# Hybrid decoder trunk on one core: gate and output steps with one engine per step, pre-split output weights, other buffers for the keys' weights

## The chip, the cores and the metric

The kernel runs on one core of a Trainium2 chip, as one program. The core has a matrix engine (PE, whose weight loads are listed apart as PEld), a vector engine (DVE), an activation engine (ACT), a general engine (POOL) and 16 DMA engines; nearly all transfers are issued in order by one queue, SP. Each engine takes its instructions in program order and waits for others on semaphores. The metric is the device time of one execution in microseconds; the median of the runs counts. A change of 0.2% is about 5 us here.

## What is computed

Two layers on x of 1024 tokens by 1024 features, all float32. Layer 0 has a dilated attention, layer 1 a gated linear attention (GLA: 4 heads, keys of 128, values of 256, chunks of 64), each followed by a squared-ReLU MLP of width 4096. Cut to what the change touches:

```python
def gla_mixer(h, w_in, w_gate_up, b_gate, norm_w, w_out):
    proj = h @ w_in                                  # q, k, v, g_out, gate_lr
    gk = gate_lr @ w_gate_up + b_gate
    log_a = jax.nn.log_sigmoid(gk) / 16.0
    b = jnp.cumsum(chunked(log_a), axis=-2)
    q_t, k_t = qc * jnp.exp(b), kc * jnp.exp(-b)
    A = causal(q_t @ k_t)                            # scores of a chunk
    U = (kc * jnp.exp(b_last - b)).T @ vc            # update of the state
    o = A @ vc + q_t @ state
    o = rmsnorm(o, norm_w) * jax.nn.silu(g_out)
    return o @ w_out

def sq_relu_mlp(h, w_up, w_down):
    a = jax.nn.relu(h @ w_up)
    return (a * a) @ w_down

for i in range(2):
    x = x + mixer[i](rmsnorm(x, norm_mix_w[i]))
    x = x + sq_relu_mlp(rmsnorm(x, norm_mlp_w[i]), mlp_w_up[i], mlp_w_down[i])
return rmsnorm(x, final_norm_w)
```

## The kernel before

**Numbers.** Every float32 operand is split into a high part and a remainder (ACT copies the high part, DVE subtracts), and a product is three matmuls of 128 x 128 weights by 512 columns. The large products go through a scheme of seven block products in place of eight, whose operands are sums and differences of blocks (a11, a12, s1 to s4, a22).

**Stages.** In order of time: attention's projection (0 to 275 us), its heads (to 870), its output projection (to 1075), the MLP of layer 0 with Up (to 1300) and Down (to 1600), the keys of the GLA with the gates of heads 0 and 1 (to 1720), the GLA's values and output gate (the object `gates`, to 1880), the two head pairs of the GLA beside its output projection (to 2050), and the MLP of layer 1 (Up to 2340, Down to the end).

**What sets the order.** The order is that of the code. Stages with a clock call `at(t, fn, priority)`, and a function runs when the clock reaches its step; `tick()` moves a clock and takes the next function of the list `steps`, so that work of ACT, DVE, POOL and SP is written between blocks of matmuls. Within a step an engine's instructions stand in the order of the calls. Tiles come from pools with a fixed number of buffers: `k4` (25 buffers of 4 KB for each partition), `t2` (8 of 2 KB), `h8`, `r6`, and eight PSUM banks. A new tile waits until the earlier user of its buffer is done, a store's landing included.

**Up of layer 0.** `Up.run` goes over 16 blocks p of seven products s (12 matmuls each). Beside product (p, s) it writes, in this order: what becomes of the product before (`done`: e is ACT's copy of pX, c11, c12 and rb are DVE's sums, then ACT's Relu and Square on them), and `stage(p + 1, s)`, which splits a piece of the next block's weights. c12 is squared ahead of the stage of s = 0, and rb ahead of that of s = 6. The object `Trickle` splits the GLA's key weights meanwhile, for later use: `Trickle.step` runs in the steps of even p + s for 4 <= p < 15, 3.5 times in each p. One head takes nine such steps: load, nothing, then cuts (ACT copies `th`, DVE subtracts `tl` one step later, SP stores both into `wp`) with differences (`less`, DVE) in the same step as the cut that reads them. `th` and `tl` are `t2` tiles, as are e and c.

**GLA gates.** `Gate` makes the decays of a head and half: first (ACT Abs, DVE min, ACT Exp and Ln, POOL subtract), second (DVE scan, POOL, three ACT Exp), third (three ACT Exp, DVE), keys, store. `Silu` makes silu of the output gate, eight pieces: load of z, first (ACT Exp, DVE add), then second (two ACT: Ln, Exp) and third (three DVE) in one step, then a store to `gscr`. All eight run in the steps of the product of `gates`.

**Pairs and output projection.** `Pair.scores(j)` makes the scores of four token blocks (16 matmuls of 128 columns in two calls of eight) into bank pA, `output(b)` makes the output of token block b for two heads, each head's matmuls followed by ACT's Square of that head (`gj`) for the norm; `flush` ends block b as `gy`, and `turn` transposes it. `Pair.load_keys` loads eight key tiles, `load_gates` the silu values. The output projection `out_proj(1)` first adds the product of heads 0 and 1, then that of heads 2 and 3. Its weights are the eight 128-row pieces of g_out: `Weights` (W) loads each raw, ACT scales it by the norm's weight into `whi`, and DVE forms `wlo`; its `prep` does so for one piece, near the place of use.

Of the kernel before, what the change touches and what calls it, by code (L numbers as in the profile page):

```python
# [19 lines left out]
P = 128  # L20
# [21 lines left out]
def hybrid_trunk(ctx, tc, x, norm_mix, norm_mlp, norm_fin, a_in, a_out, g_in, g_up, g_b, g_nw,  # L42
# [68 lines left out]
    class Weights:  # L111
        def __init__(self):
            self.slots = []
            self.scales = []
# [10 lines left out]
        def add(self, src, scale=None):  # L125
            self.slots.append(src)
            self.scales.append(scale)
# [9 lines left out]
        def prep(self, eng=pool):  # L137
            n = self.nprep
            while self.ndma <= n:
                self.dma()  # L140
            src, scale = self.raws.pop(n), self.scales[n]
            self.nprep += 1
            hi = k4(list(src.shape), F32R, "whi")
            lo = k4(list(src.shape), F32R, "wlo")
            if scale is None:
                act.activation(hi, src, AF.Copy)
                eng.tensor_tensor(lo, src, hi.bitcast(F32), op=OP.subtract)
            else:
                act.activation(hi, src, AF.Copy, scale=scale)
                dve.scalar_tensor_tensor(lo, src, scale, hi.bitcast(F32), op0=OP.mult, op1=OP.subtract)  # L150
            self.parts[n] = (hi, lo)

        def pump(self):
            while self.ndma < min(self.nprep + self.early, len(self.slots)):
                self.dma()
# [21 lines left out]
    def add_rows(w, k0, scale=None):  # L177
        for k in range(2):
            W.add(w[P * (k0 + k):P * (k0 + k + 1), :], None if scale is None else scale[:, k:k + 1])
# [428 lines left out]
    class Trickle:  # L608


        def __init__(self, out):
            self.out = out
            self.todo, self.behind = deque(), deque()
            for p in range(GH):
                self.plan(p)

        def plan(self, p):
# [9 lines left out]
            def cut(src, hi, lo, i, j):  # L627
                h, l = t2([P, 4, DK], F32R, "th"), t2([P, 4, DK], F32R, "tl")
# [11 lines left out]

            def three():
                less("b11", "b12", "b11")
                less("b12", "b22", "b12")
                cut("b11", "bh", "bl", 1, 1)

            def four():
                less("b22", "b22", "b11")
                cut("b22", "bh", "bl", 0, 0)

            def five():  # L650
                less("b21", "b21", "b22")
                cut("b12", "gh", "gl", 0, 0)
            self.todo.extend((load, lambda: None,
                              lambda: cut("b11", "ah", "al", 0, 0),
                              lambda: cut("b21", "ah", "al", 1, 1),
                              lambda: cut("b22", "d", "d", 0, 1),
                              three, four, five, lambda: cut("b21", "gh", "gl", 1, 1)))
# [16 lines left out]
    class Up:  # L674
# [165 lines left out]
        def run(self, tail):  # L840
# [44 lines left out]
    wpre = [[[drp.tile([P, 1024], F32, name=f"wp{i}_{p}_{n}") for n in PARTS] for p in range(AHEAD)] for i in range(3)]  # L885

# [657 lines left out]
    def out_proj(layer, wbc_row, o, up):  # L1544
# [10 lines left out]
        def add_block(tb, lhs, w, n, quiet=False):  # L1555
            last = tb == NB - 1 and n == 1
            ps = bank("pd")
            for k in range(4):
# [3 lines left out]
                if last:  # L1562
                    W.free(1)
            xx = xs[tb // 2][:, tb % 2, 512 * n:512 * n + 512]
            dve.tensor_tensor(xx, ps, xx, op=OP.add)
            if quiet:
                W.pump()
            else:
                tick()

        for tb in range(NB):
# [3 lines left out]
            if tb == (NB - 1 if layer else 3):  # L1575
                W.limit = 6
                W.early = RAW
            for n in range(2):
                add_block(tb, lambda k: tuple(t[k // 2][:, k % 2, 128 * tb:128 * tb + 128] for t in oT), w, n, layer == 0 and tb == NB - 1 and n == 1)
# [221 lines left out]
    gm, bgate, gnw = masks[:, 0:128].bitcast(U32), masks[:, 128:132], masks[:, 132:134]  # L1801
    low = {}

    def gate_loads():
        sp.dma_start(gm, gmask)
        sp.dma_start(bgate, g_b[0].rearrange("(h p) -> p h", p=P))
        sp.dma_start(gnw, g_nw[0].rearrange("(k p) -> p k", p=P))
# [87 lines left out]
    class Gate:  # L1895
# [10 lines left out]
        def first(self):  # L1906
            z = logits(self.h, self.half) if self.z is None else self.z
            b = bgate[:, self.h:self.h + 1]
            am = k4([P, 2, 512], F32, "ga")
            a, m = self.a, self.m = am[:, 0, :], am[:, 1, :]  # L1910
            act.activation(a, z, AF.Abs, bias=b)
            dve.tensor_scalar(m, z, b, 0.0, op0=OP.add, op1=OP.min)
            act.activation(a, a, AF.Exp, scale=-1.0)
            act.activation(a, a, AF.Ln, bias=1.0)
            pool.tensor_tensor(m, m, a, op=OP.subtract)
# [8 lines left out]
        def second(self):  # L1924
            self.eb = k4([P, 2, 512], F32, "eb")
            self.es = t2([P, 512], F32, "es")
            dve.tensor_tensor_scan(self.a, reset, self.m, 0.0, op0=OP.mult, op1=OP.add)
            e_q, e_k, e_s, a_c, m_c = self.views()
            end = [a_c[:, c, :, CH - 1:CH].to_broadcast([P, 4, CH]) for c in range(2)]
            pool.tensor_tensor(m_c[:, 0], a_c[:, 0], end[0], op=OP.subtract)  # L1930
            pool.tensor_tensor(m_c[:, 1], end[1], a_c[:, 1], op=OP.subtract)
            self.exp(e_q[:, 1], a_c[:, 1], 1.0)
            self.exp(e_k[:, 1], a_c[:, 1], -1.0)
            self.exp(e_s[:, 0], a_c[:, 0], 1.0)

        def third(self):
            e_q, e_k, e_s, a_c, m_c = self.views()
            self.exp(e_q[:, 0], m_c[:, 0], 1.0)
            self.exp(e_k[:, 0], m_c[:, 0], -1.0)
            self.exp(e_s[:, 1], m_c[:, 1], 1.0)  # L1940
            d = self.d
# [4 lines left out]
        def keys(self):  # L1946
            bs = lambda t: t.rearrange("p (b s) -> p b s", s=P)
# [15 lines left out]
        def plan(self, t, gap):  # L1963
            at(t, self.first, 7)
            at(t + gap, self.second, 7)
            at(t + gap, self.load, 8)
            at(t + 2 * gap, self.third, 7)
            at(t + 3 * gap - (gap > 1), self.keys, 8)
            at(t + 3 * gap - (gap > 1) + 1, self.store, 9)

    class Silu:
# [9 lines left out]
        def first(self):  # L1981
            d = self.d = k4([P, 2, 512], F32, "gd")
            act.activation(d, self.z, AF.Exp, scale=-1.0)
            dve.tensor_scalar(d, d, 1.0, 3e38, op0=OP.add, op1=OP.min)
# [293 lines left out]
```

## Time and profile before

| | |
|---|---|
| median of 3 runs | 2681.62 us (2680.1 to 2682.46) |
| the profiled execution | 2679.75 us, span 2678.0 us |
| around the span | 1.75 us |
| mean granted PE clock | 0.994 |
| HBM read, written | 331.09 MB, 169.54 MB |

The profiled execution is 1.87 us below the median. The profile's busy time of PE is modelled: matmuls overlap, so PE may be called busy in a stretch that has fewer matmuls than another of the same length. The count of matmuls in a stretch tells more. A row of the wait view gives who waited for whom, the total, how many waits, and the longest. A row of the view by stretches gives the stretch, its length, and for PE, PEld, DVE, ACT and POOL the busy time with the count of instructions, then the granted PE clock (1.00 is full), the share of the DMA engines that was busy, and GB/s. The chain of waits gives start, length, and what ran.

### The profile page before, as it was taken

The page shows a single profiled execution, that of the slowest core. Times are in us where ns is not written, and L with a number is a line of the kernel's source. Part 1 is how long each engine was busy: PE and PEld are TensorE (multiplying, and loading weights), DVE is VectorE, ACT ScalarE, POOL GpSimd, SP SyncE. Part 2 cuts the span into 40 slices and gives each one's busy share as a digit, 9 for nine tenths or more (in the row PEclk, how much of TensorE's full clock was granted, in tenths as well). Part 3 has the DMA queues.
Part 4 walks back from the last instruction along what each step waited for, and adds up shares of the span by engine and source line. Part 5 has one row for each costly group of instructions (what it writes and reads, how often), then busy time and mean ns, then how long its engine had stood idle before and what let it go on. Part 6 is the DMA issues. An engine that isn't in the chain of part 4 may idle for free.

```text
span 2678.0 us, 33562 instructions
## 1 busy us (share of the span) xinstructions
PE 2600.7 (97%) x12096; PEld 2151.9 (80%) x12096; DVE 1881.7 (70%) x3010; ACT 1279.6 (48%) x2340; POOL 29.3 (1%) x32
## 2 busy tenths in 40 slices
PE   8999999999999999999999999998889999999998
PEld 6888888888888888777788888876668888888886
DVE  7766878888888665666668785876556566656567
ACT  6443455555555354555544453554324455553343
POOL 0000000000000000000000000300000000000000
PEclk9999999999999999999999999999999999999999
DMA  5675455565566557666788765776414644496543
GB/s 185 240 270 185 121 142 154 140 164 147 142 159 185 186 180 269 223 216 212 280 302 302 259 220 191 259 264 221 164 41 158 253 163 145 142 327 216 184 150 124
DMA packets 351223, 528.03 MB, mean 197 GB/s; under 512 B 23408, under 2 KB 179440, under 8 KB 351056
## 3 DMA queue, kind: packets, MB, share of 16 engines
q1 hardware_dynamic: 351056, 525.88, 59.8%
q8 instruction: 95, 1.56, 0.2%
q14 instruction: 72, 0.59, 0.1%
HBM read 331.09 MB, written 169.54 MB: 187 GB/s over the span
## 4 chain that ended last, share of the span: by engine, by line
PE 74%; DVE 11%; ACT 6%; DMA 4%; issue 4%; SPq 0%; DVEq 0%; ACTq 0%
PE pB L1675 13%; PE pX L768 12%; PE pA L1675 10%; PE pV L768 8%; PE pB L967 6%; PE pY L768 4%; PE pA L967 4%; PE pZ L768 4%; PE pd L194 2%; PE pd L195 2%; PE pd L193 2%; PE pS L1072 1%; PE pO L1113 1%; DMA cw<-c 1%; DVE c L1166 1%
## 5 line engine op out<-in xcount | busy, mean ns | idle before, releaser
L1675 PE MATMUL pB<-dh 128*128 128x512 f32 x512 | 199.4, 389 | 0.0
L1675 PE MATMUL pB<-dh,dl 128*128 128x512 f32 x512 | 199.4, 389 | 0.0
L1675 PE MATMUL pB<-dl,dh 128*128 128x512 f32 x512 | 199.4, 389 | 0.0
L202 DVE TENSOR_TENSOR dl<-sin,dh 128x1024 fp32r<-128x1024 f32 x112 | 136.8, 1221 | 66.1 <-ACT dh L199 63.5
L768 PE MATMUL pV<-s4h,wd 128*128 128x512 f32 x480 | 162.0, 400 | 3.1 <-DVE rb L793 1.5
L199 ACT ACTIVATE dh<-sin 128x1024 fp32r<-128x1024 f32 x112 | 117.8, 1052 | 79.8 <-PE pB L1675 26.8
L1088 ACT ACTIVATE pt<-pt,orow 128x128 f32<-128x128 f32 (+1 forms) x192 | 85.0, 443 | 148.2 <-DVE orow L1086 146.9
L1675 PE MATMUL pA<-dh 128*128 128x512 f32 x384 | 149.7, 390 | 0.0
L1675 PE MATMUL pA<-dh,dl 128*128 128x512 f32 x384 | 149.6, 390 | 0.0
L1675 PE MATMUL pA<-dl,dh 128*128 128x512 f32 x384 | 149.6, 390 | 0.0
L199 ACT ACTIVATE dh<-kept 128x1024 fp32r<-128x1024 f32 x64 | 67.8, 1059 | 147.0 <-DVE kept L1640 105.3
L773 ACT ACTIVATE e<-pX 128x512 f32<-128x512 f32 x108 | 63.6, 589 | 112.0 <-PE pX L768 101.8
L1675 PEld LDWEIGHTS pB<-dh 128*128 128x128 f32 x512 | 96.2, 188 | 20.0
L1675 PEld LDWEIGHTS pB<-dl,dh 128*128 128x128 f32 x512 | 96.2, 188 | 19.8
L1675 PEld LDWEIGHTS pB<-dh,dl 128*128 128x128 f32 x512 | 96.2, 188 | 19.8
L768 PEld LDWEIGHTS pV<-s4h,wd 128*128 128x128 f32 x480 | 90.2, 188 | 24.0 <-DVE rb L793 3.3
L706 DVE TENSOR_TENSOR wbl<-t,wbh 128x1024 fp32r<-128x1024 f32 x48 | 58.8, 1225 | 67.2 <-ACT wbh L705 67.2
L768 PE MATMUL pX<-s3h,wgh 128*128 128x512 f32 x240 | 98.9, 412 | 6.8 <-ACT e L773 6.7
L768 PE MATMUL pX<-s2h,wbh 128*128 128x512 f32 x240 | 97.1, 404 | 8.5 <-ACT e L773 8.5
L777 ACT ACTIVATE c<-c 128x512 f32<-128x512 f32 x64 | 40.4, 631 | 128.7 <-DVE c L805 79.9
L706 DVE TENSOR_TENSOR wal<-raw,wah 128x512 fp32r<-128x512 f32 x96 | 66.0, 687 | 44.8 <-ACT wah L705 44.8
L768 PE MATMUL pY<-a12h,wah 128*128 128x512 f32 x240 | 96.0, 400 | 0.0
(328 smaller groups left out, 7428.1 us busy)
## 6 DMA issues: line engine op xcount, KB each, us to landing
sin<-acts SPq DMA_DIRECT2D x112, 512.0 KB, 4.9
acts<-s SPq DMA_DIRECT2D x64, 512.0 KB, 3.5
raw<-in_mlp_w_down_dram SPq DMA_DIRECT2D x64, 512.0 KB, 5.3
raw<-in_attn_w_in_dram SPq DMA_DIRECT2D x96, 256.0 KB, 4.4
cw<-c SPq DMA_DIRECT2D x192, 128.0 KB, 2.3
raw<-in_mlp_w_up_dram SPq DMA_DIRECT2D x48, 512.0 KB, 6.1
acts<-c SPq DMA_DIRECT2D x64, 256.0 KB, 2.2
kept<-in_mlp_w_down_dram SPq DMA_DIRECT2D x32, 512.0 KB, 6.6
```

Of the source, the lines that this page charges most:

```text
L193: pe.matmul(ps, sh, mh, start=start, stop=False)
L194: pe.matmul(ps, sh, ml, start=False, stop=False)
L195: pe.matmul(ps, sl, mh, start=False, stop=stop)
L199: act.activation(hi, src, AF.Copy)
L202: dve.tensor_tensor(lo, src, hi.bitcast(F32), op=OP.subtract)
L706: self.remain(lambda: dve.tensor_tensor(lo, src, hi.bitcast(F32), op=OP.subtract))
L768: pe.matmul(st[b], u[:, k, :], v, start=first and k + n == 0, stop=k == 3 and n == 2, skip_group_check=True)
L773: act.activation(e, self.st[p]["X"], AF.Copy)
L777: act.activation(r, r, AF.Relu)
L967: pe.matmul(self.acc[s][t], a[:, c], b[:, k, :], start=fresh and m + k + v == 0, stop=m == 1 and k == 1 and v == 2, skip_group_check=True)
L1088: act.activation(pt[:, i, :128 * n], pt[:, i, :128 * n], AF.Exp, scale=-1.0, bias=m, accum_out=self.row[:, r, HD:HD + 1])
L1675: pe.matmul(self.acc[s][t], a[:, k, c], b[:, k, :], start=fresh and m + k + v == 0, stop=m == 7 and k == 1 and v == 2, skip_group_check=True)
```

## The change

In Up of both layers, c12 and rb are still summed ahead of the stage, but their Relu and Square come after it (`add` and `squared` called apart). `Trickle` puts both parts of a cut into one `k4` tile `tb`, does each `less` one step ahead of the cut that reads it, and runs at s >= 3 for every p >= 4, four times in each p. It now also loads the eight pieces of g_out (512 KB each), splits them (ACT with the norm's scale, DVE) and stores both parts into DRAM tiles `wout` (sixteen stores of 512 KB); two steps are added to its 36. `Weights.prep` of these pieces becomes two loads of 512 KB, without work for ACT or DVE; four pieces are asked for in one place, four more at the end of the first half of the output projection, whose last token block now runs both halves of the columns side by side (`last_block`). `Gate` and `Silu` are cut so that each step has work of one engine (or of DVE then POOL). The subtraction that POOL had in `Gate.first` is part of a DVE instruction, and ACT has one more instruction there. Three of the eight `Silu`s move from the steps of `gates` into those of the output projection. `scores` and `turn` come one step later, `turn` first. In `output` the matmuls of both heads come before both Squares. `one.flush()` comes ahead of the last product of `gates`.

```diff
         def prep(self, eng=pool):
             n = self.nprep
+            self.nprep += 1
+            if isinstance(self.slots[n], tuple):
+                self.ndma = n + 1
+                got = []
+                for src, name in zip(self.slots[n], ("whi", "wlo")):
+                    t = k4([P, D], F32R, name)
+                    sp.dma_start(t.bitcast(F32), src)
+                    got.append(t)
+                self.parts[n] = tuple(got)
+                return
...
-            else:
-                act.activation(hi, src, AF.Copy, scale=scale)
-                dve.scalar_tensor_tensor(lo, src, scale, hi.bitcast(F32), op0=OP.mult, op1=OP.subtract)
...
+        def rows(self, k):
+            if k < 0:
+                return
+            raw, scale = self.raw.pop(k), gnw[:, k % 2:k % 2 + 1]
+            both = [k4([P, D], F32R, n) for n in ("whi", "wlo")]
+            act.activation(both[0], raw, AF.Copy, scale=scale)
+
+            def rest():
+                dve.scalar_tensor_tensor(both[1], raw, scale, both[0].bitcast(F32), op0=OP.mult, op1=OP.subtract)
+                for t, to in zip(both, wout[k]):
+                    sp.dma_start(to, t.bitcast(F32))
+            self.behind.append(rest)
...
             def cut(src, hi, lo, i, j):
-                h, l = t2([P, 4, DK], F32R, "th"), t2([P, 4, DK], F32R, "tl")
+                both = k4([P, 2, 4, DK], F32R, "tb")
+                h, l = both[:, 0], both[:, 1]
                 act.activation(h, r[src], AF.Copy)
...
             def three():
-                less("b11", "b12", "b11")
+                cut("b11", "bh", "bl", 1, 1)
                 less("b12", "b22", "b12")
-                cut("b11", "bh", "bl", 1, 1)
+                less("b22", "b22", "b11")
...
-                    if s == first:
+                    if s == 0:
+                        self.add(p - 1, 6)
+                    elif s == first:
                         self.done(p - 1, 6)
...
-                    if s > first and (p, s) != (3, 3):
+                    if s == 6:
+                        self.add(p, 5)
+                    elif s > first and (p, s) != (3, 3):
                         self.done(p, s - 1)
                     self.stage(p + 1, s)
+                    if s == 0:
+                        self.squared(p - 1, 6)
+                    elif s == 6:
+                        self.squared(p, 5)
...
-                    if self.side is not None and 4 <= p < NP - 1 and (p + s) % 2 == 0:
+                    if self.side is not None and 4 <= p and s >= 3:
                         self.side.step()
...
+        def last_block(w):
+            ps = [bank("pd") for _ in range(2)]
+            for k in range(4):
+                a, b = (t[k // 2][:, k % 2, 128 * NB - 128:] for t in oT)
+                wh, wl = w[k]
+                for n in range(2):
+                    mm3(ps[n], a, b, wh[:, 512 * n:512 * n + 512], wl[:, 512 * n:512 * n + 512], k == 0, k == 3)
+                W.free(1)
                 W.pump()
...
-    for t, i, q in ((7, 0, 0), (9, 1, 0), (13, 0, 1), (15, 2, 0), (17, 3, 0), (19, 1, 1), (21, 2, 1), (23, 3, 1)):
+    for t, i, q in ((7, 0, 0), (9, 1, 0), (13, 0, 1), (15, 2, 0), (17, 3, 0)):
         Silu(i, q).plan(c + t)
...
                 pe.matmul(po[:, i, :], AM[i][:, b, :], self.v(i, b), start=b == 0, stop=True, skip_group_check=True)
+            for i in range(2):
                 junk = t2([P, DV], F32, "gj")
...
-                  (24, lambda: one.scores(0)),
-                  (25, lambda: (one.turn(0), one.scores(1))),
+                  (25, lambda: (one.turn(0), one.scores(0))),
+                  (26, lambda: one.scores(1)),
```

**ACT in Up of layer 0, before.** These rows are the head of one block p, from its product 0 on: c is the piece c12 of the block before (L777 is Relu, L778 Square), L705 are the weight splits of `stage`, L629 the cuts of `Trickle`, L773 the copies e.

```order
L777 ACTIVATE c_10254<-c_10254 128x512
L778 ACTIVATE c_10254<-c_10254 128x512
L705 ACTIVATE wah<-raw 128x512
L629 ACTIVATE th<-traw 128x512
L773 ACTIVATE e_10297<-pX 128x512
L705 ACTIVATE wah<-raw 128x512
L777 ACTIVATE c_10313<-c_10313 128x512
L778 ACTIVATE c_10313<-c_10313 128x512
L629 ACTIVATE th<-traw 128x512
L773 ACTIVATE e_10341<-pX 128x512
```

The same place of the changed kernel, where L732 are the splits, L804 and L805 Relu and Square, L800 the copies, L654 the cuts of `Trickle`:

```order
L732 ACTIVATE wah<-raw 128x512
L804 ACTIVATE c_10293<-c_10293 128x512
L805 ACTIVATE c_10293<-c_10293 128x512
L800 ACTIVATE e_10328<-pX 128x512
L732 ACTIVATE wah<-raw 128x512
L804 ACTIVATE c_10344<-c_10344 128x512
L805 ACTIVATE c_10344<-c_10344 128x512
L800 ACTIVATE e_10365<-pX 128x512
L732 ACTIVATE wbh<-t 128x1024
L654 ACTIVATE tb<-traw 128x512
L654 ACTIVATE tb<-traw_10052 128x512
```

The first split stands ahead of c12's squares, and the cuts stand behind the split of wbh, none of them before the first two copies e.

**DVE ahead of the first scores, before.** gd and ge are the tiles of a `Silu` (L1993 to L1995 its third step, L1984 its first), dl the remainder of a weight split (L952), kept and raw sums of weights (L922), V the finished values (L2016), whose bank the scores take.

```order
L1993 TENSOR_TENSOR gd<-gd,ge 128x1024
L1994 SCALAR_TENSOR_TENSOR ge<-gd,ge 128x1024
L1995 SCALAR_TENSOR_TENSOR ge<-gz,ge 128x1024
L952 TENSOR_TENSOR dl<-kept,dh 128x1024
L922 TENSOR_TENSOR kept<-kept 128x1024
L1984 TENSOR_SCALAR gd<-gd 128x1024
L952 TENSOR_TENSOR dl<-kept,dh 128x1024
L922 TENSOR_TENSOR raw<-raw,kept 128x1024
L2016 TENSOR_TENSOR V<-pB,c_15683 128x512
L2016 TENSOR_TENSOR V<-pB,c_15685 128x512
L1993 TENSOR_TENSOR gd<-gd,ge 128x1024
```

The same place of the changed kernel, with L2045 to L2047 for the fourth step of a `Silu`, L990 for dl, L960 for the sums, L2072 for V and L2130 for the masking of the scores:

```order
L2045 TENSOR_TENSOR gd<-gd,ge 128x1024
L2046 SCALAR_TENSOR_TENSOR ge<-gd,ge 128x1024
L2047 SCALAR_TENSOR_TENSOR ge<-gz,ge 128x1024
L990 TENSOR_TENSOR dl<-kept,dh 128x1024
L960 TENSOR_TENSOR kept<-kept 128x1024
L990 TENSOR_TENSOR dl<-kept,dh 128x1024
L960 TENSOR_TENSOR raw<-raw,kept 128x1024
L2072 TENSOR_TENSOR V<-pB,c_15724 128x512
L2072 TENSOR_TENSOR V<-pB,c_15726 128x512
L990 TENSOR_TENSOR dl<-raw,dh 128x1024
```

No further `Silu` stands between that one and V, and none follows before the pairs. On PE the first eight score matmuls move from ahead of a product of 24 matmuls (pA from s3) to behind it.

**SP ahead of the pairs, before.** gscr is a `Silu`'s store, G the load of silu values, w_out the raw pieces of g_out (L135), xscr the residual rows.

```order
L2063 DMA G<-gscr 128x4x512
L135 DMA raw<-in_gla_w_out_dram 128x1024 x2
L1998 DMA gscr<-ge 128x2x512
L135 DMA raw<-in_gla_w_out_dram 128x1024 x2
L1998 DMA gscr<-ge 128x2x512
L1482 DMA xs<-xscr 128x1024 x4
L2049 DMA qk_m<-gks_101 128x1024
```

The same place of the changed kernel, where L143 are the loads of split pieces:

```order
L2119 DMA G<-gscr 128x4x512
L143 DMA whi<-wo_0_190 128x1024
L143 DMA wlo<-wo_1_191 128x1024
L143 DMA whi<-wo_0_192 128x1024
L143 DMA wlo<-wo_1_193 128x1024
L143 DMA whi<-wo_0_194 128x1024
L143 DMA wlo<-wo_1_195 128x1024
L143 DMA whi<-wo_0_196 128x1024
L143 DMA wlo<-wo_1_197 128x1024
L1520 DMA xs<-xscr 128x1024 x3
L2029 DMA gz<-zscr 128x2x512
```

Eight loads stand where four stood, with no store of a `Silu` among them, and the loads gz of the `Silu`s that were moved follow among those of the residual rows.

More of the change, by code (lines that the diff above doesn't have):

```diff
@@ L1961, in store, with plan @@
             sp.dma_start(to[:, 2:4, :], self.qk)
[L1963 to L1969, printed above, removed]
+        def plan(self, *when):
+            for t, fn in zip(when, (self.first, self.second, self.third, self.load, self.keys, self.store)):
+                at(t, fn, 8)
     class Silu:
@@ L2182, in hybrid_trunk @@
         else:
+            one.flush()
             gates.product(last, blocks)
@@ L2204, in hybrid_trunk @@
     one.step(3)
-    none = lambda: None
-    steps.extend([
+    later = [
         lambda: one.step(4),
@@ L2224, in hybrid_trunk, with at_step @@
         lambda: (two.flush(), t_y(2)),
-        none,
+        lambda: None,
         lambda: (t_y(3), reached.add((1, 1))),
-    ])
+    ]
+    extra = {}
+    for n, i in enumerate((1, 2, 3)):
+        for t, fn in Silu(i, 1).parts():
+            extra.setdefault(2 * n + t, []).append(fn)
+    def at_step(n):
+        later[n]()
+        for fn in extra.get(n, ()):
+            fn()
+    steps.extend([lambda n=n: at_step(n) for n in range(len(later))])
     up = Up(1)
```

123 lines of the change are left out of this document (68 added, 55 removed).

## The prediction, made before the changed kernel ran

> **What bounds the kernel now.** I read the page's totals first, then PE's waits, then a table by stretches, then the waits of the engines that PE waits for.
>
> ```profile
> PE 2600.7 (97%) x12096; PEld 2151.9 (80%) x12096; DVE 1881.7 (70%) x3010; ACT 1279.6 (48%) x2340; POOL 29.3 (1%) x32
> ```
>
> PE sets the time: its matmuls are the same in both kernels, and DVE at 70% and ACT at 48% have room. The 3% that PE is not busy understates what can be won, since matmuls overlap in the record. So I count matmuls in stretches.
>
> ```profile
> core 0: us, PE busy (x) PEld busy (x) DVE busy (x) ACT busy (x) POOL busy (x), PEclk, DMA share, GB/s
> 1075.00:1300.00 225.00, 208.05 (x886) 165.46 (x885) 150.43 (x221) 117.32 (x176) 0.64 (x2) 0.99 0.62 209
> 1775.00:1825.00 50.00, 46.87 (x196) 37.37 (x194) 37.84 (x47) 23.29 (x32) 1.19 (x2) 0.97 0.70 232
> 1825.00:1875.00 50.00, 39.16 (x184) 32.62 (x185) 33.13 (x35) 23.88 (x31) 1.91 (x2) 0.90 0.70 252
> 1875.00:1925.00 50.00, 41.55 (x182) 32.87 (x181) 30.59 (x73) 18.00 (x53) 0.00 (x0) 0.97 0.47 168
> 1925.00:1975.00 50.00, 47.18 (x237) 39.04 (x237) 22.03 (x55) 11.78 (x40) 0.00 (x0) 1.00 0.24 85
> 1975.00:2025.00 50.00, 44.26 (x193) 34.75 (x192) 29.30 (x75) 17.06 (x46) 0.00 (x0) 0.93 0.17 58
> 2100.00:2300.00 200.00, 200.00 (x883) 165.46 (x882) 126.00 (x182) 102.55 (x146) 0.00 (x0) 1.00 0.51 173
> 2350.00:2400.00 50.00, 50.00 (x222) 41.44 (x221) 28.74 (x28) 29.24 (x31) 0.00 (x0) 1.00 1.00 366
> ```
>
> The row 2100 to 2300 is Up of layer 1, at full rate: 200/883 = 0.2265 us for each matmul. At that rate Up of layer 0 (1075 to 1300) would hold 225/0.2265 = 993 and holds 886; 107 x 0.2265 = 24.2 us are lost. From 1775 to 2025 the matmuls have several shapes, so there I go by PE's waits:
>
> ```profile
> engine line waited for: us in total, times, longest us
> PE pX L768 <- ACT e L773: 15.1, 13, 2.6
> PE pO L2107 <- ACT gj L2111: 11.6, 14, 2.5
> PE pA L2073 <- DVE V L2016: 10.5, 2, 10.2
> PE pB L967 <- DVE dl L952: 3.5, 4, 2.2
> PE pT L239 <- DVE gy L2133: 2.0, 1, 2.0
> PE pO L2109 <- ACT gj L2111: 1.3, 2, 0.8
> PE pd L194 <- DVE wlo L150: 1.1, 2, 0.8
> PE pd L193 <- ACT whi L149: 1.0, 1, 1.0
> ```
>
> All of them lie where the change works. Half clock comes on top: where PEclk stands at c, a share 2(1 - c) of the stretch ran at half speed, which costs (1 - c) of it if PE had work: 1.5 us for 1775 to 1825, 1.5 for 1875 to 1925, 3.5 for 1975 to 2025. The stretches at 1.00 show that PE needs no such pauses. In 1825 to 1875 most of the half clock fell into the 10.2 us wait itself; what it cost beyond shows in the scores:
>
> ```profile
> 1856.53 3.79 PE L2073 MATMUL pA<-qq_m,qk_m 128*128 128x128 f32 x16 [10.18 <-DVE V L2016]
> 1867.07 2.05 PE pA L2073 x16
> ```
>
> The first batch of sixteen (from PE's timeline) took 3.79 us, the second (from the chain of waits) 2.05: 1.7 us.
>
> **Up of layer 0: -20.** PE waits for e, ACT's copy of pX. Why ACT is late is in its own waits, of this stage first, then of layer 1's Up:
>
> ```profile
> ACT c L777 <- DVE c L805: 35.6, 11, 4.2
> ACT th L629 <- DVE traw L639: 20.4, 8, 4.1
> ACT e L773 <- DMA wp_bh<-th: 6.0, 2, 3.1
> ACT e L773 <- DVE tl L632: 3.2, 1, 3.2
> ...
> ACT c L777 <- DVE c L805: 31.4, 9, 3.5
> ```
>
> The wait for the sum c stands in layer 1 too, 31.4 us in 200, where PE loses nothing; by itself it is harmless, and moving the squares behind the split gains nothing in layer 1. Two causes are left, both `Trickle`'s. ACT stands 20.4 us before a cut until DVE's `less` of the same step is done, with e queued behind; and e itself waits 9.2 us (6.0 + 3.2) for a `t2` buffer that a cut holds until its store has landed or its remainder is read. The change takes both away: `less` comes a step (2.72 us, 12 x 0.2265) earlier, cuts take `k4` buffers, and no cut stands ahead of the first two e. I expect 4 us to stay, since four steps in a row and the new splits still stand ahead of later e and rb: 24.2 - 4.2 = 20.
>
> The stage gets eight scalings and eight remainders, 1.13 and 1.28 us each by the rows of `whi` and `wlo` before:
>
> ```profile
> L149 ACT ACTIVATE whi<-raw,masks x8: 1132/1132/1150, 1876.8 to 2001.4; 128x1024 fp32r<-128x1024 f32 x8
> L150 DVE SCALAR_TENSOR_TENSOR wlo<-raw,masks,whi x8: 1277/1282/1285, 1879.6 to 2002.7; 128x1024 fp32r<-128x1024 f32 x8
> ```
>
> That is 9 us on ACT and 10 on DVE, hidden in a stage where they are busy 117 and 150 of 225 us; without that cover it would cost at most their sum, 19. Eight loads and sixteen stores of 0.524 MB make 12.6 MB more. The stage moved 209 x 225 = 47.0 MB at share 0.62, of which `Trickle` has 18.9 (16 loads and 56 stores of 0.262 MB; an estimate, as all its traffic is counted here). `Trickle` and the new traffic now fit into 9.5 blocks of 19.0 us, 181 us: 28.1 x 181/225 + 18.9 + 12.6 = 54.1 MB, or 299 GB/s. The last row of the table has 366 GB/s at share 1.00 with PE at full rate (x222), so I take the cost as nothing, with the rival below.
>
> **The values' stage: -4 and -10.** The waits for dl (3.5) and the half clock at 1775 to 1825 (1.5) come from `Silu`, where ACT and DVE wait for each other within a step; with one engine per step I take 4 of the 5 us. The 10.2 us wait is told by the chain of waits:
>
> ```profile
> 1834.23 8.33 DMA gscr<-ge
> 1842.58 1.07 ACT ge L1988
> 1843.67 1.07 ACT ge L1989
> 1844.77 1.24 DVE gd L1993
> 1848.43 1.22 DVE dl L952
> 1850.88 1.06 ACT dh L946
> 1854.66 1.23 DVE raw L922
> ```
>
> A store of a `Silu` took 8.33 us to land, ACT waited for its buffer, DVE for ACT, and then weights and V came in turns. The scores wait for V's bank. In the changed kernel the `Silu` has one step (5.4 us, 24 x 0.2265) between ACT's part and DVE's, and 5.4 us of products stand ahead of the scores. 10.8 us of room against a lateness of 10.2 would clear it; but dl and dh of the product that is now ahead were late as well (1848.43, 1850.88, when PE had stopped at 1846). I take 10 of 10.5 + 1.7 = 12.2 us; bounds are 4 (the product waits in the scores' place) and 12.2.
>
> The gates lose eight subtractions on POOL and get eight more instructions of 128x512 on ACT, some 0.6 us each by the nearest row:
>
> ```profile
> L773 ACT ACTIVATE e<-pX 128x512 f32<-128x512 f32 x108 | 63.6, 589 | 112.0 <-PE pX L768 101.8
> ```
>
> ACT has room for these 5 us, so they cost nothing; in front of a weight split that PE waits for they would cost up to 5.
>
> **The pairs: -11, -2, -1.** PE's timeline:
>
> ```profile
> 1895.21 0.70 PE L2107 MATMUL pO<-Sb,qq_s 128*128 128x256 f32 x2 [0.88 <-ACT gj L2111]
> 1899.36 0.98 PE L239 MATMUL pT<-ident,gy 128*128 128x128 f32 x7 [2.04 <-DVE gy L2133]
> 1903.70 0.70 PE L2107 MATMUL pO<-Sb,qq_s 128*128 128x256 f32 x2 [2.49 <-ACT gj L2111]
> ```
>
> The second head's matmuls wait for ACT's Square of the first, in the same bank. With both heads first that wait has no cause: 11.6 + 1.3 = 12.9, of which I leave 1.9 for the long ones, where ACT was late for other work. gy of the first two blocks is flushed ahead of a product of 12 matmuls (2.7 us), so its 2.0 us go. Of the half clock at 1875 to 1925, 1 us goes. Three `Silu`s come here, with three ACT instructions and four on DVE each, 1.07 and 1.24 us by the rows of ge and gd above (the fourth taken as long as the others): 10 us of ACT and 15 of DVE; in 1925 to 1975 ACT was busy for 11.8 and DVE for 22.0 of 50 us, so they hide. Without that cover they would cost up to 15.
>
> **The output weights: -4.** wlo and whi (2.1 us) and the half clock at 1975 to 2025 (3.5) go with the splits, 5.6; I leave 1.6 for late loads: the last four are asked for only as the last block frees buffers, about 5.5 us before use, and 2.1 MB at 366 GB/s take 5.7.
>
> The sum: 20 + 4 + 10 + 11 + 2 + 1 + 4 = 52 us. The profiled execution took 2679.75 us, which gives 2627.75; the median lay 1.87 above it, so I predict **2629.6 us** (-1.9%).
>
> **The rivals.**
>
> - *All goes.* Waits and half clock, 24.2 + 5.0 + 12.2 + 12.9 + 2.0 + 1.5 + 5.6 = 63.4: 2618.2. For it: layer 1's Up, with the same squares, loses nothing.
> - *The half clock stays* where no long wait led to it. Some 5 of the 52 us (1.2 at 1775, 1 in the pairs, 2.5 at the weights) are half clock that came with waits of at most 2.5 us; if it has another cause, the time is 2634.6. Against: the stretches without waits stand at 1.00. [...]
> - *The values' product waits in the scores' place, and late weights stop PE at 2000*: 6 us less from the first (4 in place of 10), 4 more lost at the second, and 1.7 of half clock: 2641.3. For it: dl and dh above were late.
> - *Up keeps most of its loss.* A `k4` buffer too is held until a store has landed, and 25 of them serve more tiles than before. Up then gains 5 instead of 20: 2644.6. Against: the pool of e itself has fewer tiles.
> - *Transfers bound Up of layer 0*, the slower one. With stores that land late, `k4` buffers come free late, ACT's splits wait for them and PE for ACT, in each block from p = 4 to 13. The 9.5 blocks take 185 us in my forecast (181 and the 4 that stay); the change is slower than before when they take over 185 + 52 = 237, that is below 54.1/237 = 228 GB/s. At 215 GB/s they take 252, which gives 2629.6 + 67 = 2696.6. For it: 209 GB/s is all that this stage has moved. Against: it did so at share 0.62, and 366 is shown.
> - *It does not do what it says*: as many waits come back elsewhere on ACT, within 5 us of 2681.6.
>
> **How the numbers follow.** My forecast has 0.45, all goes 0.12, half clock 0.08, the values and late weights 0.12, Up 0.14, transfers 0.05, nothing 0.04. A change of 0.2% is about what can be told from none. Faster: 0.45 + 0.12 + 0.08 + 0.12 + 0.14 = 0.91; slower 0.05; within, 0.04. The range goes from 2614, a little under the sum of all, to 2648, a little over Up's case; it leaves out the last two rivals and some of each edge. The bounds of 19, 15 and 5 us for work without cover would take it further up and are in the slower chance.
>
> **What would show it.** In the changed profile: Up of layer 0 holds about 975 matmuls (993 less 4.2/0.2265) in 225 us, PE's wait for e is near 2 us, and the DMA share is near 0.85 (0.62 x 225 + 12.6/0.366 us, in 205); waits of pO for gj and of pT for gy are gone or below 2 us together; the scores wait less than 2 us with PEclk above 0.97 there; no wlo or whi split in the pairs, and no PE wait on a load. Wrong would be: ACT's waits for stores of `tb` or `wo` with e behind them (Up); a wait of the product of s3 for dl or V (values); waits of pd for a landing near 2000 (weights); PEclk below 1 without a wait (half clock).

## The result, and the profile after

The changed kernel takes 2608.16 us (median of 4 runs, 2607.81 to 2610.39), the one before in the same comparison 2680.86 us: a ratio of 0.9731, with a 95% interval of 0.9715 to 0.9748. That is 72.7 us less where 52 were forecast, and below the range (2614 to 2648).

PE's waits in the changed kernel, the five largest:

```profile
PE pT L293 <- DVE xn L235: 11.9, 7, 10.4
PE pP L1137 <- ACT pt L1126: 1.2, 2, 1.1
PE pS L1110 <- DVE qT L1221: 1.1, 3, 0.4
PE pT L1351 <- DVE om L1308: 0.6, 1, 0.6
PE pB L1005 <- DVE dl L990: 0.6, 1, 0.6
```

All eight rows of before that the prediction listed are gone or under 1 us. What is left lies at the start and in layer 0's attention, outside the change. The totals of its page, then its view by stretches, columns as before, for layer 0's Up, the values and the pairs:

```profile
PE 2577.7 (99%) x12096; PEld 2148.0 (82%) x12096; DVE 1875.9 (72%) x3010; ACT 1286.3 (49%) x2348; POOL 20.2 (1%) x24
```

```profile
1075.00:1280.00 205.00, 204.49 (x902) 168.81 (x902) 160.26 (x229) 125.91 (x185) 0.64 (x2) 1.00 0.88 303
1700.00:1840.00 140.00, 140.00 (x644) 116.86 (x643) 102.60 (x133) 67.59 (x102) 9.97 (x8) 1.00 0.70 244
1840.00:1980.00 140.00, 140.00 (x698) 119.40 (x697) 94.30 (x228) 54.90 (x153) 0.00 (x0) 1.00 0.51 184
```

Up holds 902 matmuls in 205 us, 0.2273 us each, and PEclk is 1.00 in all three. The stretches need the same landmarks in both kernels, so from here a stage's length runs from one matmul of the program to another: **Up 0** from the first matmul of layer 0's output projection to the first of Down; **values** from the first matmul of that stage to the first pO from Sb; **pairs** from there to the first of layer 1's Up; **Up 1** from there to layer 1's Down.

| | before | changed | less |
|---|---|---|---|
| Up 0 | 438.1 us | 413.5 us | 24.6 |
| values | 179.3 | 158.4 | 20.9 |
| pairs | 169.4 | 143.5 | 25.9 |
| Up 1 | 306.6 | 306.4 | 0.2 |
| all else | | | 0.6 |

The spans, 2678.0 and 2605.8 us, differ by 72.2.

### The profile page after: what moved, and what is told of

The parts are those of the page before. It is cut to its first block, busy times and chain, and to the rows that moved or that the text cites. A ratio compares the mean times of both kernels' runs of the same rounds, so it can differ in the third digit from the quotient of the medians.

```text
span 2605.8 us, 33647 instructions
## 1 busy us (share of the span) xinstructions
PE 2577.7 (99%) x12096; PEld 2148.0 (82%) x12096; DVE 1875.9 (72%) x3010; ACT 1286.3 (49%) x2348; POOL 20.2 (1%) x24
## 4 chain that ended last, share of the span: by engine, by line
PE 84%; DVE 7%; DMA 3%; ACT 3%; issue 2%; SPq 0%; DVEq 0%; ACTq 0%
PE pX L795 15%; PE pB L1726 13%; PE pA L1726 10%; PE pV L795 10%; PE pB L1005 8%; PE pA L1005 6%; PE pY L795 5%; PE pZ L795 5%; PE pd L198 2%; PE pd L196 2%; PE pd L197 2%; PE pO L1151 1%; DMA cw<-c 1%; PE pS L1110 1%; DVE c L1204 1%
## 5 line engine op out<-in xcount | busy, mean ns | idle before, releaser
L205 DVE TENSOR_TENSOR dl<-sin,dh 128x1024 fp32r<-128x1024 f32 x112 | 136.6, 1219 | 63.4 <-ACT dh L202 60.9
L800 ACT ACTIVATE e<-pX 128x512 f32<-128x512 f32 x108 | 64.4, 596 | 158.6 <-PE pX L795 158.5
L795 PE MATMUL pX<-a11h,wah 128*128 128x512 f32 x240 | 95.6, 398 | 0.0
L795 PE MATMUL pV<-s1h,wbh 128*128 128x512 f32 x240 | 95.6, 398 | 0.0
```

The lines of the kernel that those rows point to most:

```text
L205: dve.tensor_tensor(lo, src, hi.bitcast(F32), op=OP.subtract)
L795: pe.matmul(st[b], u[:, k, :], v, start=first and k + n == 0, stop=k == 3 and n == 2, skip_group_check=True)
L800: act.activation(e, self.st[p]["X"], AF.Copy)
```

## The experiments

Names with u undo a part of the changed kernel; names with b add a part to the kernel before. l1_work and l1_work_sq are the kernel before with work added, more16 is the changed kernel with transfers added. The table gives each kernel's median and what its stages take **more than in the changed kernel**. The stages are read from one execution of each kernel. A stage that a run leaves alone differs by up to 0.4 us in the u runs and by up to 1.6 in the b runs and those with l1 (the pairs), and the time ahead of Up 0, in no column, by up to 3.2; so a median need not match the sum of its row.

| run | median us | Up 0 | values | pairs | Up 1 |
|---|---|---|---|---|---|
| before | 2680.86 | 24.6 | 20.9 | 25.9 | 0.2 |
| u_t2 | 2617.25 | 11.5 | 0.0 | 0.0 | 0.0 |
| u_less | 2609.88 | 2.1 | 0.0 | 0.0 | 0.0 |
| u_squares | 2637.96 | 28.2 | 0.0 | 0.0 | 0.2 |
| u_slots | 2608.91 | -0.2 | 0.0 | 0.0 | 0.0 |
| b_squares | 2654.82 | 0.9 | 20.7 | 24.3 | 0.0 |
| b_cuts | 2675.33 | 20.8 | 21.5 | 25.9 | 0.2 |
| l1_work | 2692.32 | 26.0 | 20.7 | 24.3 | 14.0 |
| l1_work_sq | 2654.89 | 1.2 | 20.4 | 25.9 | 0.0 |
| more16 | 2624.33 | 17.4 | 0.0 | 0.0 | 0.0 |
| u_scores | 2611.92 | 0.2 | 2.8 | 0.0 | 0.0 |
| u_silu_scores | 2616.18 | -0.3 | 6.3 | 2.0 | 0.0 |
| u_values_all | 2627.65 | -0.4 | 18.9 | 0.0 | 0.0 |
| u_gate | 2608.27 | -0.3 | 0.4 | 0.0 | 0.0 |
| u_heads | 2624.91 | -0.1 | 1.1 | 16.7 | 0.0 |
| u_flush | 2612.52 | -0.1 | 0.0 | 3.9 | 0.0 |
| u_weights | 2622.16 | -1.2 | 0.0 | 12.5 | 0.0 |

### Layer 0's Up: each part undone alone

u_t2:

```diff
-                both = k4([P, 2, 4, DK], F32R, "tb")
-                h, l = both[:, 0], both[:, 1]
+                h, l = t2([P, 4, DK], F32R, "th"), t2([P, 4, DK], F32R, "tl")
```

> Undoes one part: the cuts of Trickle take two t2 tiles again. Layer 0's Up lost 24.6 us before and loses nothing now. Theory (two causes that add: the buffers that cuts hold, and less in the step of its cut): the 9.2 us that ACT's copy e waited for such a buffer come back at least in part, so 4 to 9 us in this stage, with rows of e waiting for a wp store or for tl. Rival (less alone was the cause, the buffers only looked like it because less had made the cuts late): under 1 us. The other stages do not move.

u_less (each `less` again in the step of the cut that reads it, as in the kernel before):

```diff
             def three():
+                less("b11", "b12", "b11")
+                less("b12", "b22", "b12")
                 cut("b11", "bh", "bl", 1, 1)
-                less("b12", "b22", "b12")
-                less("b22", "b22", "b11")
```

> Undoes one part: each less of Trickle stands in the step of its cut again. Theory of two causes: some 12 to 18 us come back in layer 0's Up, with ACT waiting for DVE's traw ahead of e. Rival (the place of the steps, s from 3 on, keeps the cuts clear of the first two e by itself): under 4 us, since the waits for traw then fall ahead of the last e and the wd split alone.

u_squares:

```diff
-                    if s == 0:
-                        self.add(p - 1, 6)
-                    elif s == first:
+                    if s == first:
                         self.done(p - 1, 6)
...
-                    if s == 0:
-                        self.squared(p - 1, 6)
-                    elif s == 6:
-                        self.squared(p, 5)
```

> Undoes one part: c12 and rb are squared ahead of the stage again, in both layers. Theory: under 1 us in both, as layer 1's Up lost nothing before with this order. Rival (the squares in front of the splits were part of layer 0's loss): 5 us or more in layer 0, none in layer 1.

u_slots:

```diff
-                    if self.side is not None and 4 <= p and s >= 3:
+                    if self.side is not None and 4 <= p < NP - 1 and (p + s) % 2 == 0:
```

> Undoes one part: Trickle steps at even p + s for p from 4 to 14 again (39 places for 38 steps), with k4 tiles and early less kept. Theory of two causes: under 4 us in layer 0's Up. Rival (the place of the steps was the main cause): 15 us or more, with the cuts standing ahead of the first two e.

The buffers gave 11.5 us, a little over the 4 to 9 that were expected; `less` 2.1, where 12 to 18 were expected, so its rival holds; the place of the steps nothing. The squares, which I had at nothing, gave 28.2 us, more than the whole stage had lost before. ACT's timeline in u_squares at the start of one block (start, length, instruction; in brackets the idle time before it and what ended it), then DVE's:

```profile
1118.99 1.15 ACT L633 ACTIVATE whi<-raw,masks 128x1024 fp32r<-128x1024 f32 x1 [3.25 <-DMA raw<-in_gla_w_out_dram]
1120.05 1.04 ACT L804 ACTIVATE rb<-rb 128x1024 f32<-128x1024 f32 x1
1121.12 1.06 ACT L805 ACTIVATE rb<-rb 128x1024 f32<-128x1024 f32 x1
1122.09 0.61 ACT L732 ACTIVATE wd<-raw 128x512 fp32r<-128x512 f32 x1
...
1125.26 0.63 ACT L804 ACTIVATE c<-c 128x512 f32<-128x512 f32 x1 [2.04 <-DVE c L837]
1125.92 0.63 ACT L805 ACTIVATE c<-c 128x512 f32<-128x512 f32 x1
1126.46 0.61 ACT L732 ACTIVATE wah<-raw 128x512 fp32r<-128x512 f32 x1
1126.97 0.58 ACT L800 ACTIVATE e<-pX 128x512 f32<-128x512 f32 x1
```

```profile
1122.73 0.69 DVE L733 TENSOR_TENSOR wd<-raw,wd 128x512 fp32r<-128x512 f32 x1 [3.94 <-ACT wd L732]
1123.34 1.28 DVE L636 SCALAR_TENSOR_TENSOR wlo<-raw,masks,whi 128x1024 fp32r<-128x1024 f32 x1
1124.54 0.69 DVE L837 TENSOR_TENSOR c<-pV,e 128x512 f32<-128x512 f32 x1
1127.10 0.69 DVE L733 TENSOR_TENSOR wal<-raw,wah 128x512 fp32r<-128x512 f32 x1 [1.88 <-ACT wah L732]
```

This is a loop over two queues. The squares of rb stand in front of the split wd on ACT; DVE waits 3.94 us for wd, and has the sum c behind wd's remainder; ACT waits for c with wah and e behind its squares. PE's next matmul came 3.18 us late. The first row is a split of g_out that had waited for its load, so this block has two causes; the changed kernel has that late load in the same place, and PE waits 0.51 us there. Its ACT, then its DVE:

```profile
1112.59 1.15 ACT L633 ACTIVATE whi<-raw,masks 128x1024 fp32r<-128x1024 f32 x1 [3.33 <-DMA raw<-in_gla_w_out_dram]
1113.65 0.61 ACT L732 ACTIVATE wd<-raw 128x512 fp32r<-128x512 f32 x1
1114.17 1.04 ACT L804 ACTIVATE rb<-rb 128x1024 f32<-128x1024 f32 x1
```

```profile
1114.29 0.69 DVE L733 TENSOR_TENSOR wd<-raw,wd 128x512 fp32r<-128x512 f32 x1 [1.98 <-ACT wd L732]
1116.10 0.68 DVE L837 TENSOR_TENSOR c<-pV,e 128x512 f32<-128x512 f32 x1
```

With the split ahead, DVE gets wd before the squares run, and c is summed while ACT squares rb. Over the whole stage, PE's waits in u_squares are:

```profile
PE pX L795 <- ACT e L800: 13.8, 9, 3.0
PE pV L795 <- DVE rb L820: 3.5, 3, 1.4
```

### Is it the squares, or Trickle?

b_squares puts the order of the squares alone into the kernel before; b_cuts puts the `k4` cuts and the early `less` there, and leaves the squares.

> The kernel before with one part of the change alone: c12 and rb are summed ahead of the stage and squared behind it. Undoing this part alone cost 28 us in layer 0's Up. Theory A (the squares in front of the splits make ACT and DVE wait for each other at every block's start, and Trickle's work takes the slack that hides it in layer 1): this part alone gives back most of the 24.6 us, 15 us or more. Rival B (Trickle's buffers and less lost the 24.6 us, and the squares only matter once the new splits of g_out fill the stage): under 6 us.

> The kernel before with the other part alone: Trickle's cuts in k4 tiles and each less a step ahead of its cut, at the old steps and without g_out. The prediction's account (B) has this as the 20 us. Theory A: under 10 us, with c still waiting for DVE ahead of the first split in each block.

b_squares has 0.9 of the 24.6 us left, b_cuts 20.8. PE's largest wait of b_cuts outside the start is the old one:

```profile
PE pX L768 <- ACT e L773: 13.2, 13, 2.0
```

So the squares alone remove 23.7 us in the kernel before, and the two causes that the prediction named 3.8. The waits of ACT and DVE from 1075 to 1285 us tell which of them cost PE something; L805 sums c11, L810 sums c12. First the kernel before, then b_squares:

```profile
ACT c L777 <- DVE c L805: 33.1, 10, 4.2
ACT c L777 <- DVE c L810: 12.5, 9, 1.4
DVE wd L706 <- ACT wd L705: 27.5, 10, 2.9
```

```profile
ACT c L777 <- DVE c L805: 26.1, 11, 3.0
ACT th L629 <- DVE traw L639: 15.7, 7, 3.7
ACT c L777 <- DVE c L810: 0.6, 1, 0.6
DVE wd L706 <- ACT wd L705: 0.6, 1, 0.6
```

The two waits of the loop, for c12 and for wd, are gone. The wait for c11 and the one for `less` (traw) are still long, and PE loses only 0.9 us. In the changed kernel, which has the splits of g_out there too, the cuts' buffers are worth 11.5 on top. The parts don't add up; that each takes slack from the other is the likely reason, which no run shows by itself.

Why then did layer 1 lose nothing with the same order? l1_work puts into its Up what `Trickle` asks of the two engines in layer 0, without transfers, at the same steps:

```diff
+        def step(self):
+            while self.behind:
+                self.behind.popleft()()
+            src = self.up.h["a11"].parts(0)[0].bitcast(F32)
+            both = k4([P, 2, 4, DK], F32R, "tb")
+            h, l = (both[:, n].rearrange("p a b -> p (a b)") for n in range(2))
+            act.activation(h, src, AF.Copy)
+            self.behind.append(lambda: dve.tensor_tensor(l, src, h.bitcast(F32), op=OP.subtract))
...
-            self.side = Trickle(wpre[2]) if i == 0 else None
+            self.side = Trickle(wpre[2]) if i == 0 else Idle(self)
```

> The kernel before, with idle work in layer 1's Up at the steps where Trickle has it in layer 0: 39 times a copy of an operand on ACT and, a step later, a subtraction on DVE (128x512 each, results unused, no transfer). Theory A (the squares ahead of the split only cost something when more work of ACT and DVE takes the slack): layer 1's Up, which loses nothing, gets 8 us or more longer, with PE waiting for e. Rival B (it needs Trickle's transfers, landings or less): under 2 us.

> The same idle work in layer 1's Up, on the kernel before with the squares behind the stage in both layers. Theory A: under 2 us in layer 1's Up. Rival (the idle work costs by its own time, whatever the order): as long as in the run beside it.

14.0 us against 0.0. PE's wait for e covers both layers in l1_work:

```profile
PE pX L782 <- ACT e L787: 24.1, 29, 2.6
```

The order of the squares costs next to nothing while ACT and DVE have slack (0.2 us), and a second user of both, without one transfer, turns it into PE's wait. With the new order the same work is free.

### How near transfers are: more16

```diff
-                for t, to in zip(both, wout[k]):
-                    sp.dma_start(to, t.bitcast(F32))
+                for n in range(3):
+                    for t, to in zip(both, (wout, *spare)[n][k]):
+                        sp.dma_start(to, t.bitcast(F32))
```

> The changed kernel with each split piece of g_out stored three times (two copies go to tiles that nothing reads): 16.8 MB more in layer 0's Up, which moved 303 GB/s at share 0.88. That asks for 385 GB/s in 205 us. If transfers can bound this stage, it gets 10 us or more longer, with ACT or DVE waiting for landings; if the stage has room by then, under 3 us.

```profile
1075.00:1280.00 205.00, 192.09 (x826) 154.86 (x825) 151.70 (x219) 118.19 (x174) 0.65 (x2) 0.99 0.99 363
1125.00:1175.00 50.00, 45.46 (x197) 36.31 (x196) 36.01 (x52) 27.39 (x40) 0.00 (x0) 1.00 1.03 374
```

The stage grew by 17.4 us at a share of 0.99 and 363 GB/s, with PE waiting for e again (9.5 us). ACT and DVE wait for landings of the added stores and of `tb`, DVE 3.6 us at the longest. The slower rival is a real mechanism; the change stops short of it, at 0.88. A split piece is also held by three stores in place of one here, and the run doesn't tell the two apart.

### The values

u_scores puts the first scores back ahead of the product; u_silu_scores also puts the `Silu` steps together in pairs; u_values_all also takes the three moved `Silu`s back; u_gate is the old `Gate` alone. Their edits, in that order:

```diff
-                  (25, lambda: (one.turn(0), one.scores(0))),
-                  (26, lambda: one.scores(1)),
+                  (24, lambda: one.scores(0)),
+                  (25, lambda: (one.turn(0), one.scores(1))),
...
-            return ((0, self.load), (2, self.first), (3, self.second), (4, self.third), (5, self.fourth),
-                    (6, self.store))
+            return ((0, self.load), (2, lambda: (self.first(), self.second())), (3, self.third), (3, self.fourth),
+                    (4, self.store))
...
-    for t, i, q in ((7, 0, 0), (9, 1, 0), (13, 0, 1), (15, 2, 0), (17, 3, 0)):
+    for t, i, q in ((7, 0, 0), (9, 1, 0), (13, 0, 1), (15, 2, 0), (17, 3, 0), (19, 1, 1), (21, 2, 1), (23, 3, 1)):
...
-        Gate(h, half).plan(*(c + t + i for i in (0, 1, 2, 2, 4, 5)))
+        Gate(h, half).plan(c + t, 1)
```

> Undoes one part: the first scores stand ahead of the product of s3 again, with the Silu steps of one engine kept. Theory A (the scores waited because DVE and ACT waited for each other in a Silu): under 2 us in the values. Rival B (the place of the scores decides, since V's end comes at the same step in any case): 3 to 8 us, a wait of pA for V, with half clock only if it is over 2 us.

> Undoes two parts: a Silu has its ACT and DVE work of one piece in one step again (two steps in place of four), and the first scores stand ahead of the product of s3. The scores' place alone cost 2.8 us. Theory A (the Silu steps made the 10.2 us wait): 8 us or more in the values. Rival B (the three Silus that left the values, with their stores and the key loads, made it): 3 to 5 us, as with the scores alone.

> Undoes three parts: all eight Silus in the values' steps, two steps for each Silu, and the first scores ahead of the product of s3; the gates keep one engine per step. The scores and the Silu steps undone together cost 8.2 us of span in all. Theory A (the eight Silus with their stores made the wait, and the gates' part little): 15 us or more of the 20.9 us come back in the values. Theory B (the gates' steps made most of it): under 10 us.

> Undoes one part: Gate has its three mixed steps, POOL's first subtraction and its old places again. Theory A: under 2 us in the keys' and values' stages together. Theory B: 8 us or more, in front of the first scores, with PE waiting for dl.

PE's wait in u_scores, then the two of u_values_all, then the stretch of u_values_all behind its long wait:

```profile
PE pA L2129 <- DVE V L2072: 2.5, 1, 2.5
```

```profile
PE pA L2129 <- DVE V L2072: 9.6, 1, 9.6
PE pB L1005 <- DVE dl L990: 2.9, 3, 2.1
```

```profile
1825.00:1850.00 25.00, 19.93 (x101) 17.52 (x102) 17.37 (x21) 11.08 (x15) 0.00 (x0) 0.80 0.47 168
```

The three parts together bring back 18.9 of 20.9 us, among them the long wait with its half clock. Of these the place of the scores is 2.8, the `Silu` steps with it 6.3, each between the bounds of its two theories (the second run also loses 2.0 in the pairs); the other 12.6 come when the three `Silu`s stand in these steps too. So the long wait needs them: with five `Silu`s the scores waited 2.5 us at most. What the moved `Silu`s would cost with the new steps and the new place of the scores kept wasn't tried, so 12.6 holds for this order of undoing. The `Gate` steps and POOL's subtraction are worth 0.4 us at most, and the rest of the 20.9 is open.

### The pairs

u_heads puts each Square back behind its head's matmuls, u_flush leaves out the early flush, u_weights loads and splits g_out's pieces near their use again.

```diff
                 pe.matmul(po[:, i, :], AM[i][:, b, :], self.v(i, b), start=b == 0, stop=True, skip_group_check=True)
-            for i in range(2):
                 junk = t2([P, DV], F32, "gj")
...
-            one.flush()
             gates.product(last, blocks)
...
-            self.todo.extend((lambda: self.rows(KT - 2), lambda: self.rows(KT - 1)))
...
-                  (25, lambda: W.prep()),
-                  (26, lambda: W.prep()),
+                  (24, lambda: (W.dma(), W.dma())),
+                  (25, lambda: (W.dma(), W.dma())),
```

> Undoes one part: in output each head's Square stands behind its own matmuls again, ahead of the second head's. Theory: the second head waits each time until its bank is read; start to start that was 0.73 us for most of 15 blocks before, so 11 us come back in the pairs, with no half clock. The prediction's sum by the wait view (12.9 less 1.9, the long waits kept for other causes) would also give 11; if the long waits of before belong to this part, 13 or more.

> Undoes one part: gy of the first blocks is ended behind the last product of the values again. The prediction has 2 us for it. Rival (with heads first, ACT is early enough that gy is ready anyway): under 0.5 us.

> Undoes one part of the changed kernel: g_out's pieces are loaded raw and split by ACT and DVE near their use again, none of it in layer 0's Up. Theory: 4 to 8 us come back in the pairs, around the start of the second half of the output projection, with PE waiting for whi or wlo and half clock behind it; layer 0's Up keeps its time within 1 us. Rival (those waits came from ACT being late for the Squares): under 2 us in the pairs.

PE's waits of u_heads, then of u_weights:

```profile
PE pO L2163 <- ACT gj L2167: 10.6, 14, 2.7
PE pO L2165 <- ACT gj L2167: 1.4, 2, 0.8
```

```profile
PE pd L193 <- ACT whi L149: 4.1, 1, 4.1
PE pd L193 <- ACT oTh L199: 1.9, 1, 1.9
PE pT L239 <- DVE gy L2187: 1.4, 1, 1.4
PE pd L195 <- DVE oTl L202: 0.9, 1, 0.9
```

The heads' order is worth 17.8 us (1.1 of it before the landmark), where the view shows 12.0 us of waits: also the long waits, up to 2.7 us, which I had put down to other work, belong to it. The expectation had ruled out half clock; the mean granted clock, 0.999 as in the changed kernel, is too coarse to tell, as 0.001 of the span is 2.6 us.

In the changed kernel the weights are worth 12.5, over the 4 to 8 that were expected: PE waits 4.1 us for whi, and the mean granted clock of the run is 0.997 where the changed kernel has 0.999. In another place the splits stand in ACT's queue in front of oTh, the operand of the next product. The flush's wait for gy comes back as well. In the kernel before, PE waited 2.1 us for whi and wlo; so 12.5 is what late splits cost the faster pairs, and what the weights cost before wasn't measured. 17.8 + 3.9 + 12.5 is more than the 25.9 of before, so these parts overlap as those of Up do.

## Why the prediction was wrong

- **The sum's size failed twice.** My terms listed 63.4 us of loss; the three stages had 71.4. The view of PE's waits starts a wait at the modelled end of the matmul ahead. One pO wait of u_heads shows it: 0.56 us in the row, while its two matmul groups start 1.15 us apart where the changed kernel has them 0.43 apart, 0.72 lost. For Up I counted matmuls and was right (24.2 of 24.6); in the values and pairs I summed waits and half clock, 17.2 for 20.9 and 22.0 for 25.9.
- **The rests failed.** I held back 11.4 us as waits that would stay, a rest in every term but gy's. None stayed: every wait of these stages is below 1 us. "All goes", at 0.12, came nearest, and its 2618.2 is off by the same 8 us, and 2 more. The range's low edge was set from it, so it inherited the undercount.
- **Up: -20 forecast, -24.6 measured, by another cause, so that the size came near is luck.** The step that failed is "by itself it is harmless, and moving the squares behind the split gains nothing in layer 1. Two causes are left, both `Trickle`'s". The first half holds, in layer 1 only. b_squares and b_cuts show the squares at 23.7 us and the two causes at 3.8; l1_work shows why layer 1 was no witness. The row I argued from, 35.6 us for c (L805), is the wait for c11, whose place the change keeps: most of it stays in b_squares. The loop's own waits stand in layer 1 before too, 18.8 us for c12 and 24.6 for wd from 2100 to 2300 us, and cost nothing there; no row told by itself.
- **Work without cost held.** The 9 and 10 us of new splits cost Up little: without them (u_weights) it is 1.2 us shorter. Traffic came out as forecast (share 0.88 for 0.85, 303 GB/s for 299). `Gate` is worth 0.4 us at most.
- **The values: -14 forecast, -20.9 measured.** The `Silu` as the origin was right. But one engine per step was not most of it: it is 3.5 us on top of the scores' place (6.3 less 2.8), near the 4 of its own term. The term of 10 left out that three of eight `Silu`s go away, 12.6 us in the order of undoing. The scores' place, on which I spent 10 us with the `Silu` steps, is 2.8 alone.
- **The pairs: -18 forecast, -25.9 measured.** Mechanisms right, mis-sized: undone alone in the changed kernel, the heads' order is 17.8 for 11, the weights 12.5 for 4, gy 3.9 for 2. One reading was wrong: of the 3.5 us of half clock from 1975 to 2025 that I gave to the weights, 1.7 stands behind a wait of 2.01 us for gj (PEclk is 0.66 from 1996 to 2001) and belongs to the heads. The late loads that I kept 1.6 us for do not show.
- **The half clock** went with the waits (PEclk is 1.00 in all three stretches of the changed kernel), so that rival falls here.

## What to carry to other kernels

Measure a stage's loss by the distance between the same matmuls, or by their count; a list of waits is short by a little for each wait (0.56 us for 0.72 in u_heads), and by the half clock behind it (PEclk 0.66 for the 5 us behind a wait of 2.01 us, before). The longest wait of a helping engine need not be the one that costs: 26.1 us for c11 stayed where PE lost 0.9. Look for two waits that close a loop between two queues, and for what stands behind the waiting instruction on each. That a loop costs nothing in one stage is no proof for a second stage with less slack. Where a stage elsewhere runs the same code at full rate, don't keep back a rest for each term without a row that shows it.

## What the hardware showed that I had not expected

Half clock did not follow the length of one wait alone in these runs. u_flush brings back a single wait for gy, and the stage gets 3.9 us longer; the row of PE's waits, then the stretch that holds it, in which the clock stood at 0.93:

```profile
PE pT L242 <- DVE gy L2190: 2.0, 1, 2.0
```

```profile
1850.00:1875.00 25.00, 22.96 (x105) 19.36 (x104) 15.71 (x49) 7.82 (x32) 0.00 (x0) 0.93 0.77 285
```

In u_scores the wait of 2.5 us is longer, and the stretch around it stays at full clock; it cost 2.8 us:

```profile
1800.00:1825.00 25.00, 22.48 (x109) 18.59 (x108) 16.69 (x17) 9.16 (x11) 0.24 (x1) 1.00 0.66 241
```

What sets the two apart was not shown. Of u_flush's 3.9 us, some 1.75 are this half clock, an estimate from the 25 us at 0.93.
